# Encoder trunk with two attention branches: other PSUM banks for every second head's transposes, softmax sums and inverses on GpSimd

## The chip, the cores and the metric

The kernel runs on one core of a Trainium2 chip. The metric is the device time in microseconds (us) of one execution. The core has five engines with a queue of instructions each: TensorE (PE), VectorE (DVE), ScalarE (ACT), GpSimd (POOL) and SyncE (SP), which here only issues transfers.

## The reference

Two layers are applied to 256 tokens of width 1024. Each layer adds half a gated feed-forward block, then a mixing block with two kinds of attention, then half another feed-forward block. What matters here is the attention of the mixing block, 8 heads of width 64 in each branch:

```
# sliding window branch (SW): 2 key heads serve 8 query heads, with a learned sink per head
s = jnp.where(mask, q.k / sqrt(64) + bias, NEG)
m = max(s.max(-1), sink);  e = exp(s - m)
p = e / (e.sum(-1) + exp(sink - m));  o = p @ v
# neighbourhood branch (NA): 8 key heads, no sink
p = softmax(where(mask, q.k / sqrt(64) + rpb, NEG));  o = p @ v
```

## The kernel before

Tokens are two tiles of 128 rows (T = 2). Every weight is split into a high and a low part in fp32r: ACT copies the raw piece into `wh` (line 182), DVE subtracts to get `wl` (line 183), and PE multiplies three times (lines 168 to 170). The feed-forward blocks and all projections work like that, so DVE and ACT always have weight pieces to split ahead of PE's use.

In the mixing block, `ORDER` (line 45) lists the projections (Q, K, q, k, v, g) and the heads' fronts (a). PE's instructions stay in the order in which the program issues them. A planner inside the program counts PE work in ticks (one tick is three matmuls of 512 columns) and issues deferred work when it is due: a head's `turn` comes P_LAG = 10 ticks after its `front`, its `back` V_LAG = 7.5 ticks after its `turn`, and the transposes of queries and keys QK_LAG = 16 ticks after their projection. On the other engines a list scheduler puts the instructions in order when the kernel is built: of what it takes to be ready it prefers the earlier in the program, and the heads' instructions (marked `urgent`) before all others.

One head passes through these steps.

- `front` (line 537): PE computes the scores of both tiles into a bank `sc`. DVE adds the bias, writes the negated scores S to SBUF and gets each row's extreme `mx` (line 554). ACT takes the exponential in place and sums it into `sm` (line 557). For SW heads, ACT computes the sink's term `es` (line 561) and DVE adds it (line 562). DVE inverts `sm` (line 563). GpSimd multiplies S by it (line 564).
- `turn` (line 568): PE transposes the four 128x128 blocks of S into the PSUM tile `pt` (line 572). ACT copies it as `ph`, DVE subtracts to get `pl` (lines 182 and 183, by `split_to`).
- `back` (line 579): PE multiplies by the values into `po`; ACT and DVE join the parts.

PSUM has eight banks. `ps_g` holds two (`g`, for projections), `ps_acc` has two for `sc`, one for `pt` and one for `po`, and `ps_tp` has two for `tp`, which serve all other transposes: those of the normalized input (line 199), of queries (line 495), of keys (line 512; 8 heads take two banks) and of the merged result (line 711). After a key transpose ACT writes `kh` (line 514) and DVE `kl` (line 515), the last reader of that bank. The banks of a pool's tag are handed out in turn, and a new user waits for the last reader of the old one. GpSimd also computes inverse roots as powers (`rs_y`, line 174), copies the keys `kn` (line 504), and adds masks to the NA biases (`b`, line 658).

Of the kernel before, what the change touches and what calls it, by code (L numbers as in the profile page):

```python
# [11 lines left out]
F32 = mybir.dt.float32  # L12
# [4 lines left out]
ALU = mybir.AluOpType  # L17
# [4 lines left out]
P = 128  # L22
# [4 lines left out]
T = S // P  # L27
# [29 lines left out]
def hybrid_encoder(ctx, tc, x, w_gu1, w_d1, w_in, b_gate, qk_gain, rpb, sink, t5,  # L57
                   w_bna, w_bsw, w_out, w_gu2, w_d2, c_mask, c_band, out):
    nc = tc.nc

    const = ctx.enter_context(tc.tile_pool(name="const", bufs=1))
# [4 lines left out]
    ps_acc = ctx.enter_context(tc.tile_pool(name="ps_acc", bufs=1, space=PSUM))  # L66
    ps_tp = ctx.enter_context(tc.tile_pool(name="ps_tp", bufs=2, space=PSUM))
    dram = ctx.enter_context(tc.tile_pool(name="dram", bufs=1, space=DRAM))

    def pad(pool, name, nbytes):  # L70
        nc.vector.memset(pool.tile([P, nbytes // 4], F32, name=name, tag=name, bufs=1), 0.0)
# [19 lines left out]
    nc.vector.tensor_copy(ident_r, ident)  # L91
    mhalf = const.tile([P, 8], F32, name="mhalf")
    nc.vector.memset(mhalf, -0.5)
    warm = const.tile([P, 1], F32, name="warm")
    warmed = nc.scalar.activation(warm, ident[:, :1], AF.Silu)
    qkg = const.tile([P, L, 4], F32, name="qkg")
# [11 lines left out]
                                           op0=ALU.mult, op1=ALU.mult)  # L108
        nc.vector.tensor_scalar(nsnk, snk, -1.0, None, op0=ALU.mult)

    pad(const, "pad_c", 416)
    blank = ring.tile([P, 2, 512], F32R, name="blank", tag="wl", bufs=RING)
    nc.vector.memset(blank[:, 0, :].bitcast(F32), 0.0)
    idle = ps_acc.tile([P, 512], F32, name="idle", tag="po")
# [38 lines left out]
    def defer(lag, key, fn):  # L153
        later.append((now[0] + lag, len(later), key, fn))
        later.sort(key=lambda e: e[0])

    def need(*keys):
        for e in [e for e in later if e[2] in keys]:
            later.remove(e)
            e[3]()  # L160
# [16 lines left out]
    def flipped(ap):  # L177
        step, n = ap.ap[-1]
        return bass.AP(tensor=ap.tensor, offset=ap.offset + step * (n - 1), ap=[*ap.ap[:-1], [-step, n]])

    def split_to(hi, lo, src):
        linked("act", lambda: nc.scalar.activation(hi, src, AF.Copy))  # L182
        linked("dve", lambda: nc.vector.tensor_tensor(lo, src, hi.bitcast(F32), ALU.subtract))  # L183
# [286 lines left out]
    def mix(l, n, after):  # L470
        with tc.tile_pool(name="mix", bufs=1) as mp:
# [52 lines left out]
            def attend(name, ins, qT, kh, kl, kidx, bias_of, vcol, ready, oT, sink_l=None):  # L524
                oh, ol = oT
                po = [None, None]
                with tc.issue_after(rstd_done[0].ins):
                    bias = [bias_of(0), bias_of(1)]

                def urgent(fn):  # L530
                    def run(*args):
                        with tc.high_priority(500):
                            fn(*args)
                    return run

                @urgent
                def front(h):
                    need(*ins)
                    if h + 2 < NH:
                        bias.append(bias_of(h + 2))  # L540
                    b = bias.pop(0)
                    least = FMAX
                    if sink_l is not None:
                        sk, least = (v[:, sink_l * NH + h:sink_l * NH + h + 1] for v in (snk, nsnk))
                    ps = ps_acc.tile([P, T, S], F32, name="sc", tag="sc", bufs=2)
                    S_ = mp.tile([P, T, S], F32, name="S", tag="S", bufs=LAG)
                    mx = small.tile([P, T], F32, name="mx", tag="mx")
                    sm = small.tile([P, T], F32, name="sm", tag="sm")
                    for t in range(T):
                        for i, k in enumerate((kh, kl)):  # L550
                            nc.tensor.matmul(ps[:, t, :], qT[:, h, t * P:(t + 1) * P], k[:, kidx(h), :],  # L551
                                             start=i == 0, stop=i == 1)
                    for t in range(T):
                        nc.vector.tensor_tensor_reduce(S_[:, t, :], ps[:, t, :], b(t), -1.0, least,  # L554
                                                       ALU.add, ALU.min, mx[:, t:t + 1])
                    for t in range(T):
                        nc.scalar.activation(S_[:, t, :], S_[:, t, :], AF.Exp, bias=mx[:, t:t + 1], scale=-1.0,  # L557
                                             accum_out=sm[:, t:t + 1])
                    if sink_l is not None:
                        es = small.tile([P, T], F32, name="es", tag="es")  # L560
                        nc.scalar.activation(es, mx, AF.Exp, bias=sk)
                        nc.vector.tensor_tensor(sm, sm, es, ALU.add)
                    nc.vector.reciprocal(sm, sm)  # L563
                    nc.gpsimd.tensor_tensor(S_, S_, sm.unsqueeze(2).to_broadcast([P, T, S]), ALU.mult)  # L564
                    defer(P_LAG, (name, h, 0), lambda: turn(h, S_))

                @urgent
                def turn(h, S_):
                    tp = ps_acc.tile([P, T, T, P], F32, name="pt", tag="pt")
                    for t in range(T):  # L570
                        for kt in range(T):
                            nc.tensor.transpose(tp[:, kt, t, :], S_[:, t, kt * P:(kt + 1) * P], ident)  # L572
                    ph = mp.tile([P, T, T, P], F32R, name="ph", tag="ph", bufs=2)
                    pl = mp.tile([P, T, T, P], F32R, name="pl", tag="pl", bufs=2)
                    split_to(ph, pl, tp)
                    defer(V_LAG, (name, h, 1), lambda: back(h, ph, pl))

                @urgent
                def back(h, ph, pl):
                    assert ready()  # L580
                    if h % 2 == 0:
                        po[0] = ps_acc.tile([P, 2, T, P], F32, name="po", tag="po")
                        po[1] = mp.tile([P, T, P], F32, name="o", tag="o", bufs=2)
                    for kt in range(T):
                        for i, p in enumerate((ph, pl)):
                            nc.tensor.matmul(po[0][:, h % 2], vcol(kt, h), p[:, kt], start=kt + i == 0,
                                             stop=kt + i == 2)
                    a, b = (0, DH) if h % 2 == 0 else (DH, 0)
                    o, ov = po[1], flipped(po[0][:, h % 2])
                    nc.scalar.activation(o[a:a + DH], ov[b:b + DH], AF.Copy)  # L590
                    nc.vector.tensor_tensor(o[a:a + DH], o[a:a + DH], ov[a:a + DH], ALU.add)
                    if h % 2:
                        split_to(oh[:, h // 2], ol[:, h // 2], o)

                for h in range(NH):
                    yield lambda h=h: front(h)
# [79 lines left out]
            for token in ORDER.split():  # L676
                if token[0] == "a":
                    it, h = next(heads)
# [149 lines left out]
```

## Time and profile before

| what | value |
|---|---|
| median of 3 runs | 1091.73 us (1091.05 to 1091.93) |
| the profiled execution's own time | 1091.39 us |
| its span, first to last instruction | 1089.6 us |
| busy share of the span | PE 99%, DVE 79%, ACT 60%, POOL 11% |
| granted TensorE clock | 1.0 in all 40 slices |
| stretches of the heads | 218 to 312 us (first layer), 757 to 862 us (second) |

Busy time is the sum of an engine's instruction times. For PE the ends of matmuls are modelled and overlap with the next one, so PE can be slower than its pace and still show no idle time; the distance from one start to the next tells its pace. Idle time is listed before the instruction that ends it, with what released it. Lines are those of the kernel as printed above.

### The profile page before, as it was taken

To read this page: it belongs to the slowest core of one execution; us is meant where nothing else is said; L and a number is where in the kernel's file an instruction comes from. 1 tells how busy PE (TensorE), PEld (TensorE's weight loads), DVE (VectorE), ACT (ScalarE), POOL (GpSimd) and SP (SyncE) were. 2 spreads that over 40 slices of the span, in tenths; PEclk is the share of its full clock that TensorE was granted. 3 is DMA by queue.
4 is the path that set the end of the run, shared out by engine and by line. 5 is a ranking of instruction groups with operands and counts; after the bars stand their busy time and mean duration, and the time that the engine had idled before them with its cause. 6 is when DMAs were issued, how large, how long until landed. Compare 5 with 4: busy or idle time off the path is not lost.

```text
span 1089.6 us, 14660 instructions
## 1 busy us (share of the span) xinstructions
PE 1077.2 (99%) x5137; PEld 889.5 (82%) x5137; DVE 855.7 (79%) x1298; ACT 658.7 (60%) x1002; POOL 117.5 (11%) x118
## 2 busy tenths in 40 slices
PE   9999999999999999999999999999999999999998
PEld 7888878888888888888878888888888888888887
DVE  6887787889886778778777787788888767878785
ACT  6665654788764556565465565457877646656552
POOL 1400000243520000000000000003534000000000
PEclk9999999999999999999999999999999999999999
DMA  8876565755654676666657766557666555776661
GB/s 241 267 222 216 189 197 171 234 189 152 189 179 135 201 224 212 210 197 203 193 172 219 228 204 211 162 164 236 183 190 178 178 166 166 225 235 198 212 188 71
DMA packets 98827, 212.63 MB, mean 195 GB/s; under 512 B 7568, under 2 KB 13744, under 8 KB 98752
## 3 DMA queue, kind: packets, MB, share of 16 engines
q1 hardware_dynamic: 98560, 211.60, 62.1%
q8 instruction: 40, 0.66, 0.2%
q0 software_dynamic: 192, 0.08, 0.1%
q14 instruction: 35, 0.29, 0.1%
HBM read 210.59 MB, written 1.06 MB: 194 GB/s over the span
## 4 chain that ended last, share of the span: by engine, by line
PE 86%; DVE 8%; ACT 3%; issue 2%; DMA 2%; ACTq 0%; DVEq 0%
PE g L168 19%; PE g L170 19%; PE g L169 19%; PE acc L168 5%; PE acc L170 5%; PE acc L169 5%; DVE wl L183 3%; PE tp L317 2%; ACT wh L182 1%; PE tp L168 1%; PE tp L169 1%; PE tp L170 1%; PE pt L572 1%; DMA raw<-in_w_d 1%; PE sc L551 1%
## 5 line engine op out<-in xcount | busy, mean ns | idle before, releaser
L183 DVE TENSOR_TENSOR wl<-raw,wh 128x1024 fp32r<-128x1024 f32 (+1 forms) x340 | 407.8, 1216 | 68.8 <-ACT wh L182 67.5
L182 ACT ACTIVATE wh<-raw 128x1024 fp32r<-128x1024 f32 (+1 forms) x340 | 348.9, 1046 | 111.9 <-PE g L170 35.0
L168 PE MATMUL g<-wh,xh 128*128 128x512 f32 (+1 forms) x976 | 389.9, 399 | 0.0
L170 PE MATMUL g<-wh,xl 128*128 128x512 f32 (+1 forms) x976 | 379.0, 388 | 0.7 <-DVE xl L183 0.7
L169 PE MATMUL g<-wl,xh 128*128 128x512 f32 (+1 forms) x976 | 377.6, 387 | 0.4 <-DVE wl L183 0.4
L170 PEld LDWEIGHTS g<-wh,xl 128*128 128x128 f32 x976 | 183.4, 188 | 41.4 <-DVE xl L183 2.1
L169 PEld LDWEIGHTS g<-wl,xh 128*128 128x128 f32 x976 | 184.1, 189 | 32.0 <-DVE wl L183 0.8
L168 PEld LDWEIGHTS g<-wh,xh 128*128 128x128 f32 x976 | 183.6, 188 | 30.9 <-DVE hh L449 0.2
L447 ACT ACTIVATE sg<-g,rs_y 128x256 f32<-128x256 f32 x88 | 41.4, 471 | 117.1 <-PE g L170 116.8
L347 DVE TENSOR_TENSOR u<-raw 128x512 f32<-128x512 f32 x56 | 38.7, 691 | 61.9 <-DMA raw<-in_w_d 61.3
L168 PE MATMUL acc<-wh,hi 128*128 128x512 f32 x200 | 79.3, 396 | 0.0
L170 PE MATMUL acc<-wh,lo 128*128 128x512 f32 x200 | 78.0, 390 | 0.0
L169 PE MATMUL acc<-wl,hi 128*128 128x512 f32 x200 | 77.9, 390 | 0.0
L174 POOL TENSOR_TENSOR rs_y<-ms,mhalf 128x1 f32<-128x1 f32 x12 | 6.7, 556 | 660.3 <-DVE ms L220 651.9
L449 DVE SCALAR_TENSOR_TENSOR hh<-g,rs_y,sg 128x256 f32<-128x256 f32 x88 | 42.2, 480 | 38.8 <-ACT sg L447 38.7
L182 ACT ACTIVATE corner<-raw 128x512 fp32r<-128x512 f32 x28 | 17.6, 630 | 54.7 <-DMA raw<-in_w_d 38.4
L564 POOL TENSOR_TENSOR S<-S,sm 128x512 f32<-128x512 f32 x32 | 37.2, 1161 | 71.4 <-DVE sm L563 45.2
L170 PEld LDWEIGHTS acc<-wh,lo 128*128 128x128 f32 x200 | 37.6, 188 | 8.1
L169 PEld LDWEIGHTS acc<-wl,hi 128*128 128x128 f32 x200 | 37.6, 188 | 7.4
L168 PEld LDWEIGHTS acc<-wh,hi 128*128 128x128 f32 x200 | 37.6, 188 | 7.4
L557 ACT ACTIVATE S<-S,mx 128x256 f32<-128x256 f32 x64 | 32.0, 501 | 7.4 <-DVE mx L554 7.4
L317 PEld LDWEIGHTS tp<-ident,hh 128*128 128x128 f32 x176 | 24.2, 140 | 14.1 <-DVE hh L449 3.4
(190 smaller groups left out, 1477.3 us busy)
## 6 DMA issues: line engine op xcount, KB each, us to landing
raw<-in_w_gu SPq DMA_DIRECT2D x176, 512.0 KB, 4.4
raw<-in_w_d SPq DMA_DIRECT2D x100, 512.0 KB, 4.3
raw<-in_w_in SPq DMA_DIRECT2D x64, 512.0 KB, 4.3
raw<-in_w_out SPq DMA_DIRECT2D x16, 512.0 KB, 3.6
bb<-in_b_gate SPq DMA_DIRECT2D x16, 256.0 KB, 3.5
raw<-in_w_bsw SPq DMA_DIRECT2D x8, 512.0 KB, 4.0
raw<-in_w_bna SPq DMA_DIRECT2D x8, 512.0 KB, 3.5
raw<-in_w_d SPq DMA_DIRECT2D x12, 256.0 KB, 2.6
```

The lines of the kernel that those rows point to most:

```text
L168: nc.tensor.matmul(ps, xh, wh, start=first, stop=False)
L169: nc.tensor.matmul(ps, xh, wl, start=False, stop=False)
L170: nc.tensor.matmul(ps, xl, wh, start=False, stop=last)
L182: linked("act", lambda: nc.scalar.activation(hi, src, AF.Copy))
L183: linked("dve", lambda: nc.vector.tensor_tensor(lo, src, hi.bitcast(F32), ALU.subtract))
L317: nc.tensor.transpose(tp[:, SLOT[t][i], :], hh[:, i * P:(i + 1) * P], ident)
L347: sub = lambda to, x, y: nc.vector.tensor_tensor(to, x, y, ALU.subtract)
L447: nc.scalar.activation(sg, ps[:, :FC], AF.Silu, scale=rstd[t])
L449: nc.vector.scalar_tensor_tensor(hh, ps[:, FC:], rstd[t], sg, op0=ALU.mult, op1=ALU.mult)
L551: nc.tensor.matmul(ps[:, t, :], qT[:, h, t * P:(t + 1) * P], k[:, kidx(h), :], start=i == 0, stop=i == 1)
L557: nc.scalar.activation(S_[:, t, :], S_[:, t, :], AF.Exp, bias=mx[:, t:t + 1], scale=-1.0, accum_out=sm[:, t:t + 1])
L564: nc.gpsimd.tensor_tensor(S_, S_, sm.unsqueeze(2).to_broadcast([P, T, S]), ALU.mult)
```

## The change

Three things change. The power that GpSimd applies needs a constant tile of -1, and a pad shrinks by 32 bytes to make room on chip. The sum with the sink and the inverse move from DVE to GpSimd; the inverse becomes a power of -1. And odd heads put their transposes into `ps_tp` instead of the one `pt` bank, except the SW head 1.

```diff
+    minus = const.tile([P, T], F32, name="minus")
+    nc.vector.memset(minus, -1.0)
...
-    pad(const, "pad_c", 416)
+    pad(const, "pad_c", 384)
...
-                        nc.vector.tensor_tensor(sm, sm, es, ALU.add)
-                    nc.vector.reciprocal(sm, sm)
+                        nc.gpsimd.tensor_tensor(sm, sm, es, ALU.add)
+                    nc.gpsimd.tensor_tensor(sm, sm, minus, ALU.pow)
                     nc.gpsimd.tensor_tensor(S_, S_, sm.unsqueeze(2).to_broadcast([P, T, S]), ALU.mult)
...
-                    tp = ps_acc.tile([P, T, T, P], F32, name="pt", tag="pt")
+                    if h % 2 and (sink_l is None or h > 1):
+                        tp = ps_tp.tile([P, T, T, P], F32, name="pt", tag="tp")
+                    else:
+                        tp = ps_acc.tile([P, T, T, P], F32, name="pt", tag="pt")
```

## Rows read from the trace of the kernel before

**Rows 1.** The page: busy us, share of the span and instructions of each engine.
```profile
PE 1077.2 (99%) x5137; PEld 889.5 (82%) x5137; DVE 855.7 (79%) x1298; ACT 658.7 (60%) x1002; POOL 117.5 (11%) x118
```
**Rows 2.** The page: shares of the chain that ended last, by engine.
```profile
PE 86%; DVE 8%; ACT 3%; issue 2%; DMA 2%; ACTq 0%; DVEq 0%
```
**Rows 3.** Groups by line, with shapes: busy us, mean ns | idle before, releasers.
```profile
L572 PE MATMUL pt<-ident,S 128*128 128x128 f32 x128 | 19.3, 273 | 4.0 <-DVE sm L563 2.0 <-DVE pl L183 1.7 <-POOL S L564 0.2
```
**Rows 4.** PE in order of time, heads that wait: start, us [idle before, releaser].
```profile
260.83 0.63 PE L572 MATMUL pt<-ident,S 128*128 128x128 f32 x4 [0.86 <-DVE pl L183]
...
298.43 0.63 PE L572 MATMUL pt<-ident,S 128*128 128x128 f32 x4 [0.21 <-POOL S L564]
...
303.98 0.63 PE L572 MATMUL pt<-ident,S 128*128 128x128 f32 x4 [1.04 <-DVE sm L563]
...
843.07 0.63 PE L572 MATMUL pt<-ident,S 128*128 128x128 f32 x4 [1.00 <-DVE sm L563]
```
**Rows 5.** PE in order of time, 249 to 256 us: h2, keys, h3.
```profile
249.29 0.60 PE L572 MATMUL pt<-ident,S 128*128 128x128 f32 x4
...
252.75 1.03 PE L512 MATMUL tp<-ident,kn 128*128 128x128 f32 x8
...
255.45 0.39 PE L170 MATMUL g<-wh,xl 128*128 128x512 f32 x1
255.68 0.60 PE L572 MATMUL pt<-ident,S 128*128 128x128 f32 x4
```
**Rows 6.** DVE in order of time, 233 and 251 to 261 us.
```profile
233.62 1.23 DVE L183 TENSOR_TENSOR wl<-raw,wh 128x1024 fp32r<-128x1024 f32 x1
...
251.27 1.99 DVE L183 TENSOR_TENSOR wl<-raw,wh 128x1024 fp32r<-128x1024 f32 x1
...
254.92 0.15 DVE L562 TENSOR_TENSOR sm<-sm,es 128x2 f32<-128x2 f32 x1
255.10 0.42 DVE L591 TENSOR_TENSOR o<-o,po 64x256 f32<-64x256 f32 x1
...
255.96 0.15 DVE L563 RECIPROCAL sm<-sm 128x2 f32<-128x2 f32 x1
256.03 1.20 DVE L183 TENSOR_TENSOR wl<-raw,wh 128x1024 fp32r<-128x1024 f32 x1
257.15 1.40 DVE L515 SCALAR_TENSOR_TENSOR kl<-tp,qkg,kh 128x512 fp32r<-128x512 f32 x2
...
260.00 0.68 DVE L183 TENSOR_TENSOR pl<-pt,ph 128x512 fp32r<-128x512 f32 x1
```
**Rows 7.** ACT in order of time, 254 to 257 us.
```profile
254.11 1.05 ACT L182 ACTIVATE wh<-raw 128x1024 fp32r<-128x1024 f32 x1
255.06 1.26 ACT L514 ACTIVATE kh<-tp,qkg 128x512 fp32r<-128x512 f32 x2
```
**Rows 8.** Groups by line, with shapes, of POOL.
```profile
L174 POOL TENSOR_TENSOR rs_y<-hv,mhalf 128x2 f32<-128x2 f32 x4 | 2.7, 696 | 7.0 <-DVE hv L480 7.0
...
L467 POOL TENSOR_TENSOR vec<-vec,table 8x4 f32<-8x4 f32 x3 | 2.0, 680 | 0.0
...
L467 POOL TENSOR_TENSOR vec<-vec,table 8x7 f32<-8x7 f32 x2 | 0.4, 198 | 0.0
```
**Rows 9.** Busy time by stretch: us, each engine's busy time, clock, DMA share, GB/s.
```profile
218.00:312.00 94.00, 91.61 (x501) 77.37 (x500) 79.54 (x174) 73.59 (x157) 39.88 (x30) 1.00 0.59 176
```
**Rows 10.** POOL in order of time, 233 and 244 to 253 us.
```profile
233.66 2.68 POOL L174 TENSOR_TENSOR rs_y<-hv,mhalf 128x8 f32<-128x8 f32 x1 [2.33 <-DVE hv L480]
...
244.52 2.79 POOL L658 TENSOR_TENSOR b<-t,mask 128x512 f32<-128x512 f32 x2
247.26 1.04 POOL L564 TENSOR_TENSOR S<-S,sm 128x512 f32<-128x512 f32 x1
...
251.14 1.04 POOL L564 TENSOR_TENSOR S<-S,sm 128x512 f32<-128x512 f32 x1 [2.27 <-PE g L170]
```
**Rows 11.** DVE in order of time, the start.
```profile
0.88 0.07 DVE L93 MEMSET mhalf<- 128x8 f32 x1
```

## The prediction

> **What bounds the kernel now.** I read the busy table first: TensorE (PE) is busy 99% of a span of 1089.6 us [rows 1]. The chain of waits agrees: 86% of it is PE, 8% VectorE (DVE), 3% ScalarE (ACT), with no share for GpSimd (POOL) [rows 2]. PE's order is written out and the change doesn't touch it, so there are only two ways to gain or lose: the moments at which PE waits, and nothing else. Next I asked for the group that the change moves, the transposes of the softmax rows (`pt`, line 572). All 128 of them have 4.0 us of idle time before them [rows 3], and PE's list in order of time shows where it lies: five waits, at the fifth SW head (h4) of both layers, at n3 and n4 of the eight NA heads in the first layer (I call them n0 to n7), and at n4 in the second [rows 4]; the second layer's h4 repeats the first of these rows. Their idle times are 0.86, 0.86, 0.21, 1.04 and 1.00, 3.97 in all. These understate the loss: a matmul of 512 columns is drawn 0.39 long, but the next one starts 0.23 after it (255.45 to 255.68) [rows 5]. Each wait is therefore 0.16 longer than its idle time: 3.97 + 5 x 0.16 = 4.77 us. That is the whole stake of the bank change on the good side.
>
> What ends these waits? The list names three different releasers, so I compared times: h4's transposes start at 260.83, and DVE's split `pl` of h3 ends at 260.00 + 0.68 = 260.68 [rows 6], 0.15 earlier. The bank `pt` exists once, so a head's transposes must wait until the last reader of the head before, `pl`, is done. The other four waits stand at the same distance behind the `pl` of the head before. None is a wait for the scaled rows S themselves.
>
> **The banks.** After the change h3, h5, h7 and n1, n3, n5, n7 write to the two `tp` banks. Each of the five waits above is at a head whose predecessor sat in the one `pt` bank; now neighbours never share a bank, and the head two places back had its `pl` one head's time (some 5 us) earlier. All five waits go: -4.77 us.
>
> What is late next is who else uses `tp`. Before the heads this is the turn of the keys k1: eight transposes at 252.75, in two banks [rows 5]. The pool hands its banks out in turn, so h3 gets the first bank of k1. Its last reader is the first of the two `kl` on DVE, which begin at 257.15 and take 1.40 together [rows 6], so the first ends at about 257.87. With the 0.15 from split to transposes, h3 could start at 258.02. Before, it starts at 255.68, and PE does not wait there [rows 5]. New wait: 2.34 us, with PE's whole queue behind it: the scores of h5, and then the projection. It comes once in each layer. For the NA heads and for h5 and h7 the bank's reader before is a `kl` or a `pl` two odd heads back: no cost. The merges that use `tp` after the heads come behind matmuls that need n7's split anyway: no cost. h0 to h2 keep their bank. So with the engines' orders unchanged the banks give -4.77 + 2 x 2.34 = -0.09 us.
>
> **Why `kl` is so late** matters, since the change touches it. DVE stands in an unbroken queue there: sum with the sink at 254.92, `o` at 255.10, reciprocal at 255.96, a weight split `wl` at 256.03, then `kl` at 257.15 [rows 6]. The sum takes 255.10 - 254.92 = 0.18 of DVE's time and the reciprocal 256.03 - 255.96 = 0.07. Both leave for GpSimd, so `kl` comes 0.25 earlier, and each new wait is 2.34 - 0.25 = 2.09. The bounds: 2.34 if something else fills the gap; 1.22 if `kl` also goes in front of the `wl` (start 256.03, first one done at 256.75, transposes at 256.90); near zero if `kh` on ACT, at 255.06 behind a weight copy of 1.05 [rows 7], goes in front of that copy too; 2.34 + 1.12 = 3.46 if one more `wl` (256.03 to 257.15 is 1.12) goes in front. I take 2.09: `kh` ends near 255.7, before DVE turned to that `wl` at 256.03, and yet the `wl` stood first in the queue; the 0.25 taken out ahead of both gives it no reason to move back.
>
> **Sums and inverses on GpSimd.** DVE loses 16 sums and 32 reciprocals of about 0.15 each, 7.2 us of its time; PE gets nothing of that but the 0.25 above, since no PE wait is for these results. GpSimd gains 32 powers and 16 sums, all of 128x2. The power has its own row, 0.70 (128x2, x4); the sum has none: the nearest are sums on 8 partitions, 0.20 (8x7) to 0.68 on average (8x4) [rows 8]; I let it go up to 1.4, twice that. So it adds 0.70 per NA head and 0.9 to 2.1 per SW head, in all 32 x 0.70 + 16 x 0.2 to 1.4 = 26 to 45 us over two layers. In the first layer's stretch of heads GpSimd is busy 39.9 of 94 us [rows 9], so there is room. What is queued behind these waiting instructions on GpSimd: the scaling of S, the bias `b` of the next NA head, and the `rs_y` and `kn` of the keys. The place with least room is h2: two `b` from 244.52, scaling at 247.26 for 1.04, so done at 248.30 [rows 10], and its transposes at 249.29 [rows 5]: 0.99 to spare. With 0.2 + 0.7 ahead of it, it still arrives in time; with 1.4 + 0.7 it would be 1.1 late, once per layer. I take 0 (the smallest instructions of GpSimd beside free ports are the nearest case), and keep up to 2.2 for both layers. Elsewhere the results no longer stand in DVE's queue and come earlier rather than later.
>
> One rule speaks against this part. On the row: a `wl` that runs beside GpSimd's scaling at 251.14 [rows 10] takes 1.99 instead of the usual 1.20 [rows 6], a loss of 0.79 to DVE; but a `wl` that runs from 233.62, beside a power of 128x8 from 233.66, takes 1.23 [rows 6, 10]. The Trainium skill (Perfetto Trace Analysis, Optimizing Scalar/DVE Operations) says that GpSimd and VectorE share a read port into the main memory on chip, so work moved from one to the other may bring nothing. By that rule the relief of 0.25 would be lost or turned round; the row of 1.99 agrees with it for large operands, the row of 1.23 does not for small ones.
>
> The extra constant costs one memset such as that of `mhalf`, 0.07 at the start [rows 11], and a slightly smaller pad: below 0.1 us, taken as 0.
>
> **Sum.** -4.77 + 2 x 2.09 = -0.6 us. The profiled run took 1091.39 (span 1089.6 and 1.8 around it), so 1090.8 on its terms; it lies 0.34 below the median of the runs, 1091.73, so I forecast 1091.1. A difference under 0.2% (2.2 us) can't be told from no change in this kernel.
>
> **Rivals.**
> 1. The new wait is small, because the order of DVE and ACT, which is set anew for the changed kernel, brings `kl` forward. For it: `kl` is older in the program than the weight pieces that pass it, and nothing but readiness holds it back; against it: readiness was there at 256.03 and it lost. Net -4.77 + 2 x 1.22 = -2.3, down to -4.8 where no wait is left; in the middle -3.5: 1088.2.
> 2. Slower: one more `wl` passes `kl` at h3. For it: weight splits fill every gap of DVE in this stretch, and PE's wait leaves DVE without newer work. Against it: `kl` would then be ready for over 2 us. Price 2 x 3.46 - 4.77 = +2.2, 1093.9; with h2's lateness of up to 2.2 it would be 1096. It decides from a `kl` that begins later than about 258.3 on the old clock.
> 3. Shared port: each of the four small GpSimd instructions before h3's transposes (sums and powers of h3 and h4) costs DVE the 0.79 seen beside the scaling. `kl` moves back by 4 x 0.79 - 0.25 = 2.9 and both waits grow to 5.2: +5.7, 1097.4. The `wl` of 1.23 beside a power speaks against it. This is what the skill's page named above would make of it.
>
> **How the numbers follow.** Forecast (the exchange, net from -2.2 to +1.5): 0.50. Rival 1: 0.37. Rival 2: 0.09. Rival 3: 0.04. Faster by over 0.2%: 0.37; within: 0.50; slower: 0.13. The range must reach through rival 1 down to -4.8 (1086.9), and up past the forecast's own bound of +1.5: 1086.9 to 1093.2. Alone, the forecast's range is 1089.5 to 1093.2.
>
> **What would show it.** In PE's list of the new kernel, h4, n3 and n4 start without idle time in both layers; h3, behind the turn of k1, has an idle time of about 1.9 (2.09 less 0.16), released by `kl`; no transposes wait for S on GpSimd; DVE's busy time falls by about 7 us; the 128x2 powers take 0.70 and the sums near 0.2. The forecast is wrong if h3 starts without a wait (faster by more than 2.2), or if waits for GpSimd stand ahead of several heads (slower).

## The result and the profile after

The changed kernel takes 1095.49 us (median of 7 runs, 1094.31 to 1096.12) against 1091.93 for the kernel before (7 runs, 1091.05 to 1093.62): a ratio of 1.0033, 95% interval 1.0023 to 1.0042. It is slower by 3.6 us, and the forecast of 1091.1 (1086.9 to 1093.2) is missed on the upper side. The profiled execution took 1095.94, with a span of 1094.2, 4.6 more than before. The shift of work is as announced: GpSimd's busy time rose by 27.6 us and DVE's fell by 3.3 (7.6 us of sums and reciprocals left DVE, but others became longer). This is the page's busy line, to be set beside [rows 1]:

```profile
PE 1077.7 (98%) x5137; PEld 889.2 (81%) x5137; DVE 852.4 (78%) x1251; ACT 657.5 (60%) x1002; POOL 145.1 (13%) x166
```

Of all executions counted below, one of e6's eleven took 2792.35 us and is left out of its ratio.

PE has the same work and 4 us more of idle time. Who made it wait, from the view of waits of the changed kernel (us in total, times, longest):

```profile
PE pt L577 <- DVE kl L517: 3.6, 2, 1.8
PE pt L577 <- POOL S L566: 3.3, 2, 1.7
...
PE tp L497 <- DVE hv L482: 1.0, 1, 1.0
...
PE po L591 <- DVE o L596: 0.6, 2, 0.3
```

The waits of [rows 3, 4] are all gone: none of these entries is a wait for `pl`. In their place stand two waits for the scaled rows of GpSimd, two for `kl`, and smaller ones. Where they lie, from PE's list in order of time in the changed kernel (start, us, idle before it):

```profile
217.76 0.85 PE L497 MATMUL tp<-ident_r,qs 128*128 128x128 f32 x8 [0.95 <-DVE hv L482]
...
252.39 0.66 PE L577 MATMUL pt<-ident,S 128*128 128x128 f32 x4 [1.65 <-POOL S L566]
...
255.91 1.03 PE L514 MATMUL tp<-ident,kn 128*128 128x128 f32 x8
...
260.79 0.63 PE L577 MATMUL pt<-ident,S 128*128 128x128 f32 x4 [1.80 <-DVE kl L517]
...
309.93 0.39 PE L591 MATMUL po<-ph,va 128*128 128x256 f32 x1 [0.29 <-DVE o L596]
```

The transposes at 252.39 are h2's, those at 260.79 h3's; both waits repeat in the second layer (1.65 at 792.79, 1.80 at 801.20). Each idle time is 0.16 short of the loss, as in the prediction. So h2 costs 2 x 1.81, h3 2 x 1.96, the query transposes of the first layer 1.11, and a `po` of an NA head 0.45 in each layer: 9.55 us. Less the old 4.77 this is +4.8, of a span that grew by 4.6. The 1.11 belongs to this one execution: the traces of e1, e3, e5, e6, e7, e9 and e10 below, which have the same sums and inverses on GpSimd, show no idle time at these transposes. Without it the sum is +3.7, and the medians differ by 3.6.

Why h2 waits is in GpSimd's list in order of time:

```profile
245.35 1.19 POOL L663 TENSOR_TENSOR b<-t,mask 128x512 f32<-128x512 f32 x1
246.49 0.20 POOL L564 TENSOR_TENSOR sm<-sm,es 128x2 f32<-128x2 f32 x1
246.65 1.65 POOL L663 TENSOR_TENSOR b<-t,mask 128x512 f32<-128x512 f32 x1
248.24 0.61 POOL L506 COPY kn<-kn 128x512 f32<-128x512 f32 x1
248.81 0.70 POOL L565 TENSOR_TENSOR sm<-sm,minus 128x2 f32<-128x2 f32 x1
251.04 0.30 POOL L564 TENSOR_TENSOR sm<-sm,es 128x2 f32<-128x2 f32 x1 [1.53 <-ACT es L563]
251.30 1.03 POOL L566 TENSOR_TENSOR S<-S,sm 128x512 f32<-128x512 f32 x1
252.30 1.68 POOL L565 TENSOR_TENSOR sm<-sm,minus 128x2 f32<-128x2 f32 x1
254.06 1.04 POOL L566 TENSOR_TENSOR S<-S,sm 128x512 f32<-128x512 f32 x1
```

The reader is to follow the heads through the lines. The sum at 246.49 and the power at 248.81 are h2's; with them done at 249.51, h2's scaling (line 566) could begin. It doesn't: the next instruction in the queue, at 251.04, is the sum of h3. That one waits 1.53 us for ACT's sink term of h3, and h2's scaling, which needs nothing any more, stands behind it until 251.30. It ends at 252.33, and PE goes on at 252.39. GpSimd's list shows it working in the order of its queue, and that order was made when the kernel was built.

h3's wait is the one that was foreseen. DVE's and ACT's lists of the changed kernel at that place:

```profile
258.25 1.73 DVE L185 TENSOR_TENSOR wl<-raw,wh 128x1024 fp32r<-128x1024 f32 x1 [0.33 <-ACT wh L184]
259.91 1.40 DVE L517 SCALAR_TENSOR_TENSOR kl<-tp,qkg,kh 128x512 fp32r<-128x512 f32 x2
```

```profile
258.12 1.25 ACT L516 ACTIVATE kh<-tp,qkg 128x512 fp32r<-128x512 f32 x2
```

The first `kh` is done at 258.75, but `kl` stands behind a weight split until 259.91, as in [rows 6]. The split is longer than there, 1.73 instead of 1.20; the experiments come back to this.

### The profile page after: what moved, and what is told of

Its sections match the earlier page's. It is cut to its first block, busy times and chain, and to the rows that moved or that the text cites. A ratio compares the mean times of both kernels' runs of the same rounds, so it can differ in the third digit from the quotient of the medians.

```text
span 1094.2 us, 14631 instructions
## 1 busy us (share of the span) xinstructions
PE 1077.7 (98%) x5137; PEld 889.2 (81%) x5137; DVE 852.4 (78%) x1251; ACT 657.5 (60%) x1002; POOL 145.1 (13%) x166
## 4 chain that ended last, share of the span: by engine, by line
PE 83%; DVE 8%; ACT 3%; issue 3%; DMA 2%; POOL 1%; ACTq 0%; DVEq 0%
PE g L172 18%; PE g L170 18%; PE g L171 18%; PE acc L170 5%; PE acc L172 5%; PE acc L171 5%; DVE wl L185 4%; PE tp L319 2%; ACT wh L184 2%; PE tp L171 1%; PE tp L172 1%; PE tp L170 1%; PE po L591 1%; PE sc L553 1%; PE pt L577 1%
```

## The experiments

All runs of one group were timed beside the kernel before on the same chip; times are medians, ratios are to the kernel before with their 95% intervals.

| kernel | time, us | before | ratio (interval) | waits of `pt` per layer, with the 0.16 |
|---|---|---|---|---|
| changed kernel | 1095.49 | 1091.93 | 1.0033 (1.0023 to 1.0042) | h2 1.81, h3 1.96 |
| e1, scaling ahead of the next sum | 1095.59 | 1091.34 | 1.0043 (1.0029 to 1.0057) | h3 3.17 |
| e2, banks alone | 1093.32 | 1091.34 | 1.0020 (1.0011 to 1.0030) | h3 2.36 |
| e3, sums alone | 1096.51 | 1091.34 | 1.0051 (1.0039 to 1.0064) | h2 1.81, h4 0.61, n3 0.85, n4 1.20 |
| e4, even heads in tp | 1086.92 | 1091.34 | 0.9962 (0.9949 to 0.9974) | none |
| e5, e4 with sums in e1's order | 1088.00 | 1091.58 | 0.9972 (0.9961 to 0.9983) | none |
| e6, e4 with sums as changed | 1091.28 | 1091.58 | 0.9994 (0.9985 to 1.0003) | h2 1.8 |
| e7, changed, h3 in pt | 1092.78 | 1091.58 | 1.0015 (1.0006 to 1.0024) | h2 1.8, h4 0.61 |
| e9, e1 with scores first | 1098.72 | 1091.58 | 1.0071 (1.0057 to 1.0084) | h3 3.86 |
| e10, e1 with keys first | 1098.52 | 1090.93 | 1.0063 (1.0049 to 1.0077) | none by a bank |
| e11, e2 with keys first | 1098.53 | 1090.93 | 1.0062 (1.0049 to 1.0076) | none by a bank |

**e1: the order on GpSimd.**

```diff
+                scaled = []
...
-                        nc.gpsimd.tensor_tensor(sm, sm, es, ALU.add)
+                        with ExitStack() as order:
+                            if scaled:
+                                order.enter_context(tc.issue_after(scaled[-1].ins))
+                            nc.gpsimd.tensor_tensor(sm, sm, es, ALU.add)
                     nc.gpsimd.tensor_tensor(sm, sm, minus, ALU.pow)
-                    nc.gpsimd.tensor_tensor(S_, S_, sm.unsqueeze(2).to_broadcast([P, T, S]), ALU.mult)
+                    scaled.append(nc.gpsimd.tensor_tensor(S_, S_, sm.unsqueeze(2).to_broadcast([P, T, S]), ALU.mult))
```

> The changed kernel with one more issue order: on GpSimd, a head's scaling of S goes in front of the next head's sum with the sink. Only h2's scaling and h3's sum change places, once per layer. Theory A (order): h3's sum stood in front and waited for ACT's sink term, so h2's transposes waited 1.81 us in each layer. Expected: power of h2 done near 249.5, scaling done near 250.6, wait of h2 about 0.1 each; 1095.5 - 3.4 = 1092.1 us, h3's wait for kl (1.95 each) stays. Rival B (length): GpSimd's longer queue itself (two b, kn, sum, power) makes h2 late; then h2 still waits 1 us or more and the time stays above 1094. Rival C (port): GpSimd's new instructions slow DVE; then nothing changes, 1095.5.

Of all queues only these two instructions change places, once per layer. GpSimd's list of e1:

```profile
247.51 0.70 POOL L569 TENSOR_TENSOR sm<-sm,minus 128x2 f32<-128x2 f32 x1
248.29 1.04 POOL L570 TENSOR_TENSOR S<-S,sm 128x512 f32<-128x512 f32 x1
249.74 0.72 POOL L568 TENSOR_TENSOR sm<-sm,es 128x2 f32<-128x2 f32 x1 [0.41 <-ACT es L564]
```

The scaling follows its power at once, and h2's transposes start at 249.38 without idle time: theory A is right about the cause of h2's wait, and rival B is out. But the time did not fall: 1095.59, 3.5 above what was expected. In the first layer PE starts its last matmul before h3 at 255.62 instead of 258.61, 2.99 earlier (1.81 of it from h2, 1.11 from the query transposes, which don't wait here). The first `kl` starts at 258.13 instead of 259.91, only 1.78 earlier. So h3's wait grew by the difference, from 1.96 to 3.17. A second cost comes on top in the second layer. PE's list of e1, and its stretches with the granted clock (the column after the busy times), the first of them from the first layer:

```profile
799.45 0.63 PE L581 MATMUL pt<-ident,S 128*128 128x128 f32 x4 [3.03 <-DVE kl L517]
799.83 0.95 PE L554 MATMUL sc<-skT,sqT 128*128 128x256 f32 x4
800.57 0.63 PE L170 MATMUL g<-wh,xh 128*128 128x512 f32 x1
801.00 0.63 PE L171 MATMUL g<-wl,xh 128*128 128x512 f32 x1
```

```profile
260.00:261.00 1.00, 1.00 (x7) 0.82 (x6) 1.00 (x4) 0.56 (x2) 0.00 (x0) 1.00 0.92 338
...
800.50:801.50 1.00, 1.00 (x5) 0.81 (x4) 0.77 (x4) 0.33 (x2) 0.00 (x0) 0.50 0.88 328
...
804.50:805.50 1.00, 1.00 (x7) 0.83 (x6) 0.32 (x1) 0.00 (x0) 0.38 (x1) 1.00 0.00 0
```

After 3.03 us without work the granted clock is 0.50, which is the 1.2 GHz level, and matmuls follow each other by 0.43 instead of 0.23. In the first layer, after a wait of 3.01, it stayed at 1.00. The two waits at h3 and two of 0.45 at a `po` make 7.3 us, 2.5 more than the old 4.77, of a span that is 4.2 longer; by an estimate from the clock's rows, the slow stretch adds 1.7. The time is the one that rival C named, but not in its way, since h2's wait went. The port isn't out, though: it shows at h3, under e9.

**e2 and e3: one part alone.** e2 has the diff's bank lines alone, e3 its lines for sums and inverses alone.

> Only the bank part: odd heads to the two tp banks, sums and inverses on DVE as before. Theory A: the five old waits go (-4.77 us) and h3 waits for kl in both layers, about 2.3 us each without the relief of DVE: 1091.9 us, the same as before; no wait at h2. Rival: the wait for kl is a product of the sums on GpSimd; then h3 waits under 1 us and the time is near 1088.

> Only the sums and inverses on GpSimd, all heads' transposes in the one pt bank. Theory A: h2 waits 1.8 us for GpSimd in each layer, as in the changed kernel; of the five old waits those at n3 and n4 stay, those at h4 shrink, since h2's wait gives DVE 1.8 us to catch up and its queue is shorter: 1091.9 + 3.6 - (0 to 2) + about 1 at the first layer's query transposes = 1094 to 1096. Rival: moving the sums alone relieves DVE and costs nothing; 1091 to 1092, h2 without a wait.

e2's only waits of `pt` are h3's. PE's list of e2:

```profile
257.98 0.63 PE L575 MATMUL pt<-ident,S 128*128 128x128 f32 x4 [2.20 <-DVE kl L515]
```

2.36 with the 0.16, where the prediction's working had 2.34 without the relief of DVE. The profiled run of e2 has a span of 1088.9 and took 1090.72, 0.7 below the kernel before's profiled run. Its median is 2.0 above, though (1.4 above what was expected), and its runs spread from 1090.72 to 1096.74. Three of the eleven have a mean granted clock of 1.000, and take 1090.72, 1092.03 and 1092.09, within 0.8 of the kernel before's median either way: there the exchange came out as worked out. The other eight have 0.997 or 0.998 and take 1092.37 to 1096.74. That the clock falls there after h3's wait is likely but not shown, since the one trace of e2 is of a run at 1.000. The changed kernel, with no wait over 2 us in the profile, kept 1.000 in all seven runs.

e3 has h2's wait of 1.81 without any change of banks, so it belongs to the sums. In the groups by line, its `pt` has 7.7 us of idle time:

```profile
L574 PE MATMUL pt<-ident,S 128*128 128x128 f32 x128 | 19.4, 274 | 7.7 <-DVE pl L185 4.4 <-POOL S L566 3.3
```

Both rivals fall: the wait at h3 needs no sums, and the sums alone cost 5.2 us, 0.5 more than the upper end of what was expected.

**e4: the other heads get the tp banks.**

```diff
-                    tp = ps_acc.tile([P, T, T, P], F32, name="pt", tag="pt")
+                    if h % 2 == 0 and (sink_l is None or h > 3):
+                        tp = ps_tp.tile([P, T, T, P], F32, name="pt", tag="tp")
+                    else:
+                        tp = ps_acc.tile([P, T, T, P], F32, name="pt", tag="pt")
```

> Sums on DVE as before; the two tp banks go to the even heads from h4 on (h4, h6, n0, n2, n4, n6), all others use pt. Neighbours still never share a bank from h3 on, and the first head in a tp bank is h4, 5 us after h3, when both kl have been done. Theory A: all five old waits go and none comes: 1091.9 - 4.8 = 1087.1 us. Rival (given back later): without those waits PE runs into the next late result (a po or pt of a later head), and a third or more of the 4.8 comes back: 1088.7 or more.

1086.92, ratio 0.9962 (0.9949 to 0.9974): 4.4 us faster, as expected, and the fastest version of this study. Its `pt` group has no idle time left, against 4.0 in [rows 3]:

```profile
L575 PE MATMUL pt<-ident,S 128*128 128x128 f32 x128 | 19.1, 272 | 0.0
```

Its span is 4.9 shorter than before, where the old waits were 4.77: nothing of the gain is given back later.

**e5, e6 and e7: the parts put together.** e5 and e6 have e4's condition; e5 has the order of e1, e6 the sums as in the change. e7 is the changed kernel with `h > 3` in place of `h > 1`.

> The banks of e4 (even heads from h4 on in tp) with the sums and inverses on GpSimd in the order of e1. Theory A (sums on GpSimd are neutral once nothing waits for them): no wait at h2, h3, h4, n3, n4; the time of e4, 1086.9, within 1 us. Rival B (relief): DVE's 7 us less work lets PE run faster somewhere; 1085.5 or less. Rival C (port or later results): GpSimd's small instructions delay other results, as at the first layer's query transposes (1.11 us once in the changed kernel) and at po (0.45 each); 1088.5 or more.

> The banks of e4 with the sums and inverses on GpSimd in the order of the changed kernel (h3's sum in front of h2's scaling). Theory A: only h2's wait of 1.81 us per layer is left of the big ones: e5's time + 3.6, so about 1090.5 to 1092. Rival: with pt handed over earlier the wait at h2 is covered elsewhere; then it is within 1.5 us of e5.

> The changed kernel with h3 in pt as before (h5, h7 and the odd NA heads stay in tp). h2's wait of 1.81 stays, h3's wait for kl (1.95 each) goes, and h4 waits for the pl of h3 again, 0.6 each as in e3. Theory A: 1095.5 - 3.9 + 1.2 = 1092.8 us. Rival: PE is held at h3 or h4 by DVE's queue whatever the bank; then h4's wait is about 1.9 and the time stays near 1095.5.

e5 and e6 differ in GpSimd's order alone, and by 3.3 us: that is h2's wait, twice, now with nothing behind it that could take its place. e7 hits 1092.8. Between e4 and e5 lie 1.1 us in the wrong direction for the sums, but the intervals overlap. In e5's trace a `po` of an NA head has idle time in each layer, as in the changed kernel, which e4's has not: two waits of 0.42. Whether the sums on GpSimd cost anything once they are in good order is not settled; no gain from them shows.

**e9: an attempt on h3's longer wait.** Weight pieces issued after h4's front were put behind h4's scores on DVE:

```diff
-        split_to(wh[:, :nk, :n], wl[:, :nk, :n], r)
+        with ExitStack() as order:
+            if held:
+                order.enter_context(tc.issue_after(held[-1].ins))
+            split_to(wh[:, :nk, :n], wl[:, :nk, :n], r)
...
+                        scored = nc.vector.tensor_tensor_reduce(S_[:, t, :], ps[:, t, :], b(t), -1.0, least,
+                                                                ALU.add, ALU.min, mx[:, t:t + 1])
+                    if sink_l is not None and h == 4:
+                        held.append(scored)
```

> e1 with one more issue order: weight pieces that are issued after the front of h4 come behind the scores of h4 in DVE's queue (in e1 a weight split stands in front of them, in the kernel before behind them). Theory A: e1's wait of 3.17 at h3 is 0.8 longer than with the banks alone (2.36), because that weight split delays the scores, then ACT's exponentials, its next weight copy and kh; with the scores first the wait is 2.1 to 2.4 each, and the granted clock, which fell to half after the wait of 3.19 in the second layer, falls less often: 1095.6 - 2 x 0.9 - (0 to 1.3) = 1092.5 to 1093.8. Rival: the 0.8 comes from the weight split that takes 1.72 instead of 1.2 beside GpSimd's scaling; then the wait stays near 3 and the time near 1095.5.

It got worse: 3.86 per layer, and 1098.72, and the clock fell after both waits. The order moved further than meant: two weight splits now stand together shortly before `kl`, with only `o` and a `va` between, and the two take 3.19 us, where two undisturbed ones take 2.35. So the run tells neither theory from the other. But the traces of e1 and e2 have the shares. e1's list of DVE, then of GpSimd:

```profile
256.48 1.72 DVE L185 TENSOR_TENSOR wl<-raw,wh 128x1024 fp32r<-128x1024 f32 x1 [0.33 <-ACT wh L184]
258.13 1.40 DVE L517 SCALAR_TENSOR_TENSOR kl<-tp,qkg,kh 128x512 fp32r<-128x512 f32 x2
```

```profile
256.08 1.04 POOL L570 TENSOR_TENSOR S<-S,sm 128x512 f32<-128x512 f32 x1
```

And e2's:

```profile
255.97 1.20 DVE L183 TENSOR_TENSOR wl<-raw,wh 128x1024 fp32r<-128x1024 f32 x1
257.09 1.40 DVE L515 SCALAR_TENSOR_TENSOR kl<-tp,qkg,kh 128x512 fp32r<-128x512 f32 x2
```

```profile
256.22 1.85 POOL L564 TENSOR_TENSOR S<-S,sm 128x512 f32<-128x512 f32 x1 [4.10 <-ACT kh L514]
```

The transposes of k1 start at 252.91 in e1 and at 252.69 in e2. Counted from them, `kl` starts 5.22 later in e1 and 4.40 later in e2: 0.82. Of this 0.29 is a split that starts later, behind ACT's copy, and 0.53 is the split's length. In e2 the split starts before h4's scaling and the scaling takes 1.85; with the sums on GpSimd the scaling starts first and the split takes 1.72. No run changes one share alone.

**e10 and e11: `kl` first.** Weight pieces loaded after the turn of k1 were put behind its `kh` and `kl`, in e1 and in e2:

```diff
+            for inst in held:
+                order.enter_context(tc.issue_after(inst.ins))
...
+                    if key == "k1":
+                        held[:] = [copied, split]
```

> e1 with an issue order that puts the weight pieces loaded after the turn of k1 behind that turn's kh on ACT and kl on DVE; banks and sums as in e1. Theory A: h3's wait (3.17 in e1, 3.86 in e9) is nothing but kl standing behind weight splits in DVE's queue; with kl first it starts within 1 us of the end of kh, h3 waits under 0.5 us, the clock doesn't fall, and the time is that of e5, 1088.0, within 1 us. Rival: h3 waits for the bank in another way (kh late on ACT, or the whole turn); then more than 1.5 us of wait stays per layer and the time is 1092 or more.

> The banks alone (e2: 1093.3, with h3 waiting 2.36 per layer) with the same issue order for kh and kl; sums on DVE. Theory A: no wait at h3 and none of the five old ones: the time of e4, 1086.9, within 1 us. Rival: the weight splits pushed behind kl come late for the next projection, and PE waits there instead; 1089 or more.

h3 waits for no bank any more in both, so its wait was indeed `kl`'s place in the queue. But the time is 1098.5 in both: e11's rival was right. PE's list of e10, a few us before h3:

```profile
255.58 0.50 PE L174 MATMUL g<-wh,xh 128*128 128x512 f32 x1 [2.10 <-ACT wh L188]
256.92 0.50 PE L175 MATMUL g<-wl,xh 128*128 128x512 f32 x1 [0.84 <-DVE wl L189]
```

The weight pieces that now stand behind `kl` were needed by the very next projection. The edit moved more than the one split in front of `kl`: in e2 four stand before it, from 249.02 on, the last at 255.97; in e11 none does after 243 us. DVE's list of e11, then PE's:

```profile
253.93 1.41 DVE L519 SCALAR_TENSOR_TENSOR kl<-tp,qkg,kh 128x512 fp32r<-128x512 f32 x2
255.45 3.50 DVE L187 TENSOR_TENSOR wl<-raw,wh 128x1024 fp32r<-128x1024 f32 x3
```

```profile
255.47 0.50 PE L172 MATMUL g<-wh,xh 128*128 128x512 f32 x1 [2.10 <-ACT wh L186]
256.73 0.79 PE L173 MATMUL g<-wl,xh 128*128 128x512 f32 x1 [0.76 <-DVE wl L187]
...
257.75 0.63 PE L172 MATMUL g<-wh,xh 128*128 128x512 f32 x1
258.18 0.63 PE L173 MATMUL g<-wl,xh 128*128 128x512 f32 x1
```

The last two start 0.43 apart, and the granted clock is 0.50 from 257 to 261 us. It falls in both layers of e11 and in the first of e10, and is part of the cost: e11's waits for these pieces are 4.2 and 1.9 us in all, and its span is 12.4 longer than e4's. An order that moves the last split alone was not run, so it isn't shown that DVE has no room there. Of the choices that were run, not needing `kl` early, which is what e4 does, is the one that gains.

## Why the prediction was wrong

- **The five old waits go (-4.77).** Right: none is left in the changed kernel, and e4, where nothing else changes, gains 4.4 us.
- **h3 waits for `kl` (2.34, less a relief of 0.25).** Right in place. The size, 1.96 against 2.09, was luck: the relief has the wrong sign. With h2 out of the way (e1) the wait is 3.17, longer than with the sums on DVE (2.36); 0.53 of that comes from h4's scaling, which now starts before the split in front of `kl`. In the changed kernel h2's wait stood before h3's and hid that: there `kl` starts 4.00 after k1's transposes, in e1 5.22.
- **h2's scaling on GpSimd ("I take 0", at most 1.1 per layer).** This is the step that failed: 1.81 in each layer, 3.6 of the 5.4 us between the forecast's sum (-0.6) and the trace's (+4.8). I bounded it by durations, as if the power and the sum stood directly before their own scaling. What cost the time was an order that the sum did not have to have: h3's sum, itself waiting for ACT, in front of h2's finished work. The prediction named what is queued behind the waiting instructions on GpSimd, the scaling of S first of all, but priced only the time that the new instructions work and not the time that they wait. e1 and the pair e5, e6 show it. It was not the only one: e1, which has no such wait, still takes 1095.59, by the relief of the wrong sign and by the clock.
- **"Elsewhere the results come earlier rather than later."** Mostly; but two `po` waits of 0.45 are new. They show in every version here that has both the sums on GpSimd and heads in the `tp` banks, and in none that has only one of the two; their cause stays open. The sums and powers also took longer than the signs named, 0.25 and 0.90 on average instead of 0.2 and 0.70, and DVE's busy time fell by 3.3 instead of 7:

```profile
L565 POOL TENSOR_TENSOR sm<-sm,minus 128x2 f32<-128x2 f32 x32 | 28.8, 899 | 15.6 <-ACT S L559 14.6
...
L564 POOL TENSOR_TENSOR sm<-sm,es 128x2 f32<-128x2 f32 x16 | 4.1, 254 | 29.3 <-ACT es L563 29.3
```

- **The port (rival 3, 0.04).** Not as priced, but not absent: beside h4's scaling the split before `kl` takes 1.73 instead of 1.20. The row against the port was misread. The split of 1.23 at 233.62 started 0.04 before the power of 128x8 [rows 6, 10], and it was the power that paid: 2.68 instead of the 1.64 that it takes undisturbed.
- **Rival 2** had the right sign and, with h2's lateness, nearly the right time (1096), but the wrong place: no second split passed `kl`; the queue that blocked was GpSimd's.

## What to carry to other kernels

A small operation that moves to a queue worked in order costs the wait that it brings along, for all that stands behind it; look for the one instruction that waits for another engine in front of work that is ready, and fix the order by hand. A bank borrowed from a pool is worth what its last reader allows: with the sums on DVE the same three banks cost 2.0 us (e2) or gained 4.4 (e4), depending on which heads took them. And where another engine's queue sets the next wait, taking away the wait before it can move time instead of saving it (e1).

## What the runs showed of the hardware

**A GpSimd instruction that starts behind a DVE split waits for it.** In the changed kernel the power of 128x8 that the query transposes needed, in the execution that was traced (GpSimd's list first, then DVE's):

```profile
209.81 3.68 POOL L176 TENSOR_TENSOR rs_y<-hv,mhalf 128x8 f32<-128x8 f32 x1 [1.05 <-DVE hv L482]
```

```profile
209.64 2.35 DVE L185 TENSOR_TENSOR wl<-raw,wh 128x1024 fp32r<-128x1024 f32 x2
```

And in the kernel before:

```profile
209.36 1.64 POOL L174 TENSOR_TENSOR rs_y<-hv,mhalf 128x8 f32<-128x8 f32 x1 [0.27 <-DVE hv L480]
```

```profile
209.47 2.36 DVE L183 TENSOR_TENSOR wl<-raw,wh 128x1024 fp32r<-128x1024 f32 x2 [0.20 <-ACT wh L182]
```

Started 0.17 after the first of two splits, the power ends 1.50 after the last of them (211.99 to 213.49); started 0.11 before them, it takes 1.64, and the splits take as long as ever. The power at 233.66 [rows 10], 0.04 behind a split, likewise ends 1.49 after it (234.85 to 236.34). So a shift of 0.3 us in who starts first made the wait of 1.11 in this one execution. The large scaling, started first, does hold a split up, by 0.79 [rows 6, 10]. The Trainium skill (SBUF — State Buffer, SBUF: two separate sides) says that of a GpSimd instruction and a DVE one with two inputs there, whichever starts first has the shared port pair for its whole instruction and the other is blocked. The trace agrees where DVE is first and where GpSimd's operand is large; a power on 128x8 did not block the splits that began after it.

**The granted clock can fall after a few us of waiting in a kernel that is otherwise full, and not each time.** It fell to 0.50 after both of e9's waits (3.70 us idle); after one of e1's two (3.03, but not 3.01); and around two waits with one matmul between them, in both layers of e11 (2.10 and 0.76, 2.10 and 0.71) and in one of e10's (2.10 and 0.84 both times). It stayed at 1.00 after e2's two waits of 2.20 in the run that was traced.
